# Layer 2 of a two-layer decoder trunk: two heads' projections ahead of the fast-multiplication sets, and head chains begun by a count of steps

## The chip, the cores and the metric

The kernel runs on one core of one Trainium2 chip. The metric is device time in microseconds (us) of one launch. Engines are named as in the profile: PE is TensorE's matmuls, PEld its weight loads, DVE VectorE, ACT ScalarE, POOL GpSimd, SP SyncE. SP and POOL also issue the large transfers, each through a queue of its own.

## The reference, cut to what matters

Two layers run on x of 512 positions by 2048 channels. The first (a convolution branch and an attention branch) isn't touched. The second is a gated linear recurrence with 16 heads:

```python
h = rmsnorm(x, od_norm_g)
p = h @ od_w_in                                # 2048 -> 4 x 2048
q, f_raw, i_val, g = _split(p, ...)            # each 16 heads of 128
o = hgrn2(q, f_raw, i_val, lb, hgrn_norm_g) * jax.nn.silu(g)
x = x + o @ od_w_out
return rmsnorm(x, final_norm_g)

# in hgrn2, of each head, in chunks of 64 positions:
logf = logaddexp(log(lb), log1p(-lb) + log_sigmoid(f_raw))
k = -expm1(logf)
A = einsum('bhtk,bhsk,bhtsk->bhts', q, k, decay)
o = A @ v + (q * exp(b)) @ state               # then rmsnorm per head
```

Everything is float32 and has to be that accurate, so each matrix product is made of three passes on TensorE over operands that are split into a high and a low part: high by high, high by low, low by high.

## The kernel before, in words

**A quarter.** `mm3` (L221 to L223) issues three matmuls of 128 x 128 by 512 columns. Twelve of them are a quarter: one 128 x 512 strip of weights against four row blocks of x. A weight tile (512 KB, two quarters) comes from one of several makers. `Loaded` (L162, L166, L167) fetches the tile with a transfer of POOL's queue as `wh`, has ACT write its negative to `wl`, and fetches the tile again, added to `wl`: what is left is the low part. `Formed` loads raw blocks through SP, forms sums of them on DVE, and splits them with one ACT and one DVE instruction (L248, L249). The tiles stand in one list, `items`. `begin(n)` makes the second step of tile n + 2 and the first of tile n + 3 whenever tile n is begun, so the work on a tile starts three tiles ahead of its use. High and low parts have four and three slots.

**Ticks.** After each quarter (or product, below) `tick()` lets every running chain make one step. A chain is a Python generator; it emits the small operations of a head, of a mean square and so on, between the big matmuls. `finish(...)` steps the named chains to their end at once, without big matmuls between the steps.

**Order.** TensorE's instructions run in the order in which the code is written. The other engines' are ordered by the framework's scheduler.

**Layer 2 before.** Layer 1's last output projection calls `to_h1(c)` for each of 16 column blocks c: it stores x to DRAM (`xd`, L794), splits it into `h1` (L244, L245) and squares it (L256). Then the projections to v and to the gate come first. They are computed in four sets, from weight blocks of 512 KB, by a Strassen-Winograd scheme: seven half-size products (28 weight tiles, each of 12 matmuls) in place of eight. A set has four passes: A11 and A12 (8 tiles), S1 and S2 (8), S4 and S3 (8), A22 (4), where S1 = A21 + A22, S2 = S1 - A11, S3 = A11 - A21, S4 = A12 - S2 are sums of quadrants of x. The sums are made in the first pass of the first set: `x_sums(k)` (L828 to L836) reloads two blocks of x from `xd`, scales them on ACT, makes four sums on DVE, and splits them; S1 goes into the half of `h1[k]` in which A21 would stand. The first set's tiles of pass one are `Loaded`; all other set tiles are `Formed`. Before the third pass of the last set `restore()` (L757) loads A21 back and splits it into `h1`, since the heads need the whole of x.

Then the 16 heads follow: `head(h)` computes the queries ("oq", 4 quarters, L1098) and the decays ("of", 4 quarters, L1102 to L1107), and spawns the chain `hgrn` (L1000 to L1087; 14 steps, the last of them the four transposes of L1087, which wait for `on`, the gated output, L1083). The output projection `w_out` is done by groups of four heads. Group 0 is spread over heads 5 to 7 and group 1 over heads 9 to 11, after a `finish` of the heads that they need; group 2 comes after head 15. The loading of x for the residual (`load_xa`) is spawned at the start of the heads.

Of the kernel before, what the change touches and what calls it, by code (L numbers as in the profile page):

```python
# [49 lines left out]
def trunk(ctx: ExitStack, tc: tile.TileContext, x, w, ws, vec, cst, rope, msk, out, order):  # L50
# [622 lines left out]
    ph = [None]  # L673
# [52 lines left out]

    for s_ in range(len(SETS)):
        for m in range(4):
            if s_ == 0:
                items.append(Loaded(ws[0, 0, 0, m]))  # L730
                items.append(Loaded(ws[0, 1, 0, m]))
            else:
                items.append(Formed(lambda s_=s_, m=m: t1_raw(s_, m), lambda r: r[0], lambda r, s_=s_, m=m: t1_sum(s_, m)))
                items.append(Formed(lambda s_=s_, m=m: block(s_, 1, 0, m), lambda r: r))
# [15 lines left out]
    for i in range(N_EARLY, N_WTILES):  # L750
        items.append(Loaded(w[i]) if 2 * i < LAST else Kept(w[i], 2 * i - LAST))
# [10 lines left out]
    with ectx as cctx:  # L762
# [60 lines left out]
    def x_sums(k):  # L823

        t = ring("xr")
        u = t.rearrange("p (a c) -> p a c", a=2)
        for a in range(2):
            nc.sync.dma_start(u[:, a, :], xd[:, k + 8 * a, :])  # L828
            act.activation(u[:, a, :], u[:, a, :], AF.Copy, scale=vs[:, V_ODG + k + 8 * a:V_ODG + k + 8 * a + 1])
        a11, a21, a12, a22 = u[:, 0, :H], u[:, 0, H:], u[:, 1, :H], u[:, 1, H:]  # L830
        q = ring("xs")
        s1, s2, s3, s4 = [q[:, i * H:(i + 1) * H] for i in range(4)]
        dve.tensor_tensor(out=s1, in0=a21, in1=a22, op=ALU.add)
        dve.tensor_tensor(out=s2, in0=s1, in1=a11, op=ALU.subtract)
        dve.tensor_tensor(out=s3, in0=a11, in1=a21, op=ALU.subtract)
        dve.tensor_tensor(out=s4, in0=a12, in1=s2, op=ALU.subtract)  # L836
        split_plain(s1, h1[k][0][:, H:], h1[k][1][:, H:])
        split_plain(q[:, H:], *sums[k])

    def operand(name, k):  # L840
        if name in ("A11", "S1"):
            return [t[:, (name == "S1") * H:][:, :H] for t in h1[k]]
        if name in ("A12", "A22"):
            return [t[:, (name == "A22") * H:][:, :H] for t in h1[k + 8]]
        i = int(name[1]) - 2
# [21 lines left out]
    rh = fp.tile([P, 4], F32, name="rh")  # L867
# [17 lines left out]
    def keep(tag, b):  # L885
        return fp.tile([P, S], F32, name=tag, tag=f"{tag}{b}")

    for s_ in range(4):
        p1, p2 = banks(), banks()
        for m in range(4):  # L890
            product(p1, "A11", m)
            if s_ == 0:
                x_sums(2 * m)
                t1_raw(0, m)
            product(p2, "A12", m)
            if s_ == 0:
                x_sums(2 * m + 1)
                t1_sum(0, m)
        if s_ == 0:
            finish(c1)  # L900
            dve.tensor_scalar(rh, r1, 0.5, None, op0=ALU.mult)
# [6 lines left out]
        for m in range(4):  # L908
            product(p5, "S1", m)
            product(p6, "S2", m)  # L910
        u = [keep("u", b) for b in range(2)]
# [5 lines left out]
        if s_ == 3:  # L917
            restore()
# [7 lines left out]
        for b in range(2):  # L926
            result(s_, 1, 2 + b, p7[b], u[b])
        p4 = banks()
# [10 lines left out]
    spawn(load_xa(xd))  # L939
# [151 lines left out]
    heads = []  # L1091

    def head(h, fill):
        gate = tp.tile([P, S], F32, name="gate", tag="gate", bufs=2)
        nc.sync.dma_start(gate.rearrange("p (b c) -> p b c", b=4), gd[h // 4][:, :, blocks(h % 4)])
        ps = dense("oq", h, h1)
        q = hgt("q")
# [171 lines left out]
```

## Time and profile before

| | us |
|---|---|
| median of three runs (1833.5 to 1834.43) | 1834.14 |
| the profiled execution | 1832.11 |
| its span, first to last instruction | 1830.2 |
| PE busy, of the span | 1753.9 (96%) |
| DVE busy | 1193.8 (65%) |
| ACT busy | 734.6 (40%) |
| POOL busy | 239.2 (13%) |
| chain of waits: PE's share of the span | 83% |

The mean granted TensorE clock of the run is 0.976 of full speed (2.4 GHz; the lower level, 0.50, is 1.2 GHz). An engine's busy time says nothing on the rate at which TensorE worked: at the lower clock a matmul is busy twice as long. So a stretch of a program in which TensorE is the bound loses two things, the idle time, and half of the time that it was busy at the lower clock. Both are read from one row of a table by stretches: the width less the busy time times the granted clock.

### The profile page before, as it was taken

To read this page: it belongs to the slowest core of one execution; us is meant where nothing else is said; L and a number is where in the kernel's file an instruction comes from. 1 tells how busy PE (TensorE), PEld (TensorE's weight loads), DVE (VectorE), ACT (ScalarE), POOL (GpSimd) and SP (SyncE) were. 2 spreads that over 40 slices of the span, in tenths; PEclk is the share of its full clock that TensorE was granted. 3 is DMA by queue.
4 is the path that set the end of the run, shared out by engine and by line. 5 is a ranking of instruction groups with operands and counts; after the bars stand their busy time and mean duration, and the time that the engine had idled before them with its cause. 6 is when DMAs were issued, how large, how long until landed. Compare 5 with 4: busy or idle time off the path is not lost.

```text
span 1830.2 us, 22277 instructions
## 1 busy us (share of the span) xinstructions
PE 1753.9 (96%) x8227; PEld 1451.7 (79%) x8227; DVE 1193.8 (65%) x2258; ACT 734.6 (40%) x1345; POOL 239.2 (13%) x310
## 2 busy tenths in 40 slices
PE   8999999999999999976999999899899899999997
PEld 6888888888788888854888887788688788878887
DVE  8554867586799765647777786266555555556766
ACT  6334444443433322545454554233233323223344
POOL 5000000000000000340000000222122222222200
PEclk9999999999999999987999999999899999999998
DMA  6222222222552232498676775977577867877752
GB/s 235 83 93 87 89 89 88 92 86 93 182 158 93 94 102 98 155 264 250 205 227 230 203 225 154 296 170 162 133 160 167 181 148 167 168 168 155 155 136 93
DMA packets 96524, 280.68 MB, mean 153 GB/s; under 512 B 9632, under 2 KB 23200, under 8 KB 95520
## 3 DMA queue, kind: packets, MB, share of 16 engines
q0 software_dynamic: 29952, 109.07, 28.1%
q1 hardware_dynamic: 65888, 169.24, 27.3%
q8 instruction: 64, 1.05, 0.2%
q10 hardware_dynamic: 576, 0.97, 0.2%
q14 instruction: 44, 0.36, 0.1%
HBM read 259.31 MB, written 19.92 MB: 153 GB/s over the span
## 4 chain that ended last, share of the span: by engine, by line
PE 83%; DVE 6%; DMA 5%; issue 3%; ACT 2%; POOL 1%; POOLq 0%; DVEq 0%; ACTq 0%; SPq 0%
PE mm L223 23%; PE mm L222 23%; PE mm L221 23%; PE aux L988 2%; PE aux L222 2%; PE aux L221 2%; PE aux L223 2%; DMA rw<-ws 2%; PE aux L454 1%; DVE wl L249 1%; PE aux L1035 1%; DVE hl L245 1%; DMA wh<-w 1%; DMA wl<-w 1%; DVE wq L249 1%
## 5 line engine op out<-in xcount | busy, mean ns | idle before, releaser
L248 ACT ACTIVATE wq<-raw 128x512 fp32r<-128x512 f32 x256 | 161.0, 631 | 351.0 <-PE mm L223 341.5
L221 PE MATMUL mm<-hh,wq 128*128 128x512 f32 x656 | 263.0, 401 | 2.3 <-ACT wq L248 2.3
L249 DVE TENSOR_TENSOR wq<-raw,wq 128x512 fp32r<-128x512 f32 x256 | 183.7, 720 | 120.1 <-ACT wq L248 119.5
L223 PE MATMUL mm<-hh,wq 128*128 128x512 f32 x656 | 257.4, 392 | 2.8 <-DVE wq L249 2.8
L222 PE MATMUL mm<-hl,wq 128*128 128x512 f32 x656 | 256.8, 391 | 0.0
L166 ACT ACTIVATE wl<-wh 128x1024 fp32r<-128x1024 f32 x96 | 101.6, 1058 | 298.8 <-PE mm L223 249.9
L221 PE MATMUL mm<-hh,wh 128*128 128x512 f32 x512 | 210.1, 410 | 0.0
L223 PE MATMUL mm<-hh,wl 128*128 128x512 f32 x512 | 203.3, 397 | 6.4 <-DMA wl<-w 6.4
L222 PE MATMUL mm<-hl,wh 128*128 128x512 f32 x512 | 202.7, 396 | 0.0
L503 DVE SCALAR_TENSOR_TENSOR y<-u,cwh,y 128x512 f32<-128x512 f32 x240 | 178.7, 749 | 2.4
L223 PEld LDWEIGHTS mm<-hh,wq 128*128 128x128 f32 x656 | 123.8, 189 | 30.4 <-DVE wq L249 3.9
L221 PEld LDWEIGHTS mm<-hh,wq 128*128 128x128 f32 x656 | 124.3, 190 | 27.9 <-ACT wq L248 2.8
L222 PEld LDWEIGHTS mm<-hl,wq 128*128 128x128 f32 x656 | 124.2, 189 | 25.9 <-DVE hl L245 0.5
L223 PEld LDWEIGHTS mm<-hh,wl 128*128 128x128 f32 x512 | 98.0, 191 | 29.0 <-DMA wl<-w 7.4
L222 PEld LDWEIGHTS mm<-hl,wh 128*128 128x128 f32 x512 | 98.4, 192 | 18.8
L221 PEld LDWEIGHTS mm<-hh,wh 128*128 128x128 f32 x512 | 98.5, 192 | 18.5
L664 DVE TENSOR_TENSOR xall<-xall,mm 128x512 f32<-128x512 f32 x96 | 65.7, 684 | 67.6 <-PE mm L223 67.5
L221 PE MATMUL mm<-mh,wq 128*128 128x512 f32 x256 | 101.6, 397 | 0.0
L222 PE MATMUL mm<-ml,wq 128*128 128x512 f32 x256 | 101.3, 396 | 0.0
L223 PE MATMUL mm<-mh,wq 128*128 128x512 f32 x256 | 101.2, 395 | 0.0
L162 POOL DMA_DIRECT2D wh<-w x88 | 49.7, 565 | 334.2 <-PE mm L223 288.1
L167 POOL DMA_DIRECT2D wl<-w x88 | 76.8, 873 | 95.1 <-ACT wl L166 88.6
(309 smaller groups left out, 3627.1 us busy)
## 6 DMA issues: line engine op xcount, KB each, us to landing
raw<-w SPq DMA_DIRECT2D x127, 512.0 KB, 3.3
rw<-ws SPq DMA_DIRECT2D x92, 512.0 KB, 4.7
wh<-w POOLq DMA_DIRECT2D x88, 512.0 KB, 3.7
wl<-w POOLq DMA_DIRECT2D x88, 512.0 KB, 6.0
ts<-ws POOLq DMA_DIRECT2D x16, 512.0 KB, 5.6
xall<-xT SPq DMA_DIRECT2D x16, 256.0 KB, 4.7
xd<-xall SPq DMA_DIRECT2D x16, 256.0 KB, 2.5
wh<-ws POOLq DMA_DIRECT2D x8, 512.0 KB, 6.9
```

What stands on the lines that cost most here:

```text
L162: pool.dma_start(self.hi, self.src)
L166: act.activation(self.lo, self.hi.bitcast(F32), AF.Copy, scale=-1.0)
L167: pool.dma_start(self.lo, self.src, accum_op=ALU.add)
L221: pe.matmul(ps, a[0][:, asl], b[0][:, bsl], start=first, stop=False)
L222: pe.matmul(ps, a[0][:, asl], b[1][:, bsl], start=False, stop=False)
L223: pe.matmul(ps, a[1][:, asl], b[0][:, bsl], start=False, stop=last)
L245: dve.scalar_tensor_tensor(out=lo, in0=src, scalar=g, in1=hi.bitcast(F32), op0=ALU.mult, op1=ALU.subtract)
L248: act.activation(hi, src, AF.Copy)
L249: dve.tensor_tensor(out=lo, in0=src, in1=hi.bitcast(F32), op=ALU.subtract)
L503: dve.scalar_tensor_tensor(out=y, in0=u[:, j:j + S], scalar=cwh[:, w0 + j:w0 + j + 1], in1=y, op0=ALU.mult, op1=ALU.add)
L664: dve.tensor_tensor(out=xa[c], in0=xa[c], in1=ps, op=ALU.add)
L988: pe.matmul(ps[:, i * 192:(i + 1) * 192], ks[:, blocks(g)], rhs, start=True, stop=True)
```

## The change

Three things change in layer 2; what is computed stays, up to the order of the same products.

1. *Two heads first.* Queries and decays of heads 0 and 1 (16 quarters) come right after layer 1, before the sets. Their eight tiles are `Loaded`; the first set's pass-one tiles become `Formed` like those of the other sets. `x_sums` runs under head 0's quarters and takes x from where it still stands on the chip, without loads; it makes S1, S2 and S4. The finished queries and key factors go to DRAM (`qd`) and come back when the heads start.
2. *S3 takes S1's place.* S3 is made by `x_diff` in the first and second pass of the first set, from four loads of 512 KB, and is what stands in the half of `h1`. So `restore()` can come after the third pass of the last set, before the fourth. The first two tiles of the heads after the sets are loaded by SP and split on ACT and DVE (`plain`).
3. *Chains by count.* A hook, called at every tick, begins the next head's chain 8 ticks after the last one (10 for the sixth to the twelfth), provided that its q and k are there. The queries and decays of a head therefore run one or two heads ahead of its chain. `w_out` of group 0 is spread over heads 6 to 9 and of group 1 over heads 9 to 12.

```diff
+    hooks = []
     def tick():
+        for f in hooks:
+            f()
         for g in list(chains):
...
+    for i in range(N_EARLY, N_EARLY + 8):
+        items.append(Loaded(w[i]))
     for s_ in range(len(SETS)):
         for m in range(4):
-            if s_ == 0:
-                items.append(Loaded(ws[0, 0, 0, m]))
-                items.append(Loaded(ws[0, 1, 0, m]))
-            else:
...
+    for i in range(N_EARLY + 8, N_WTILES):
+        if i < N_EARLY + 10:
+            items.append(Formed(lambda i=i: plain(i), lambda r: r))
...
     def x_sums(k):
-        t = ring("xr")
-        u = t.rearrange("p (a c) -> p a c", a=2)
+        u = xt.tile([P, 2, S], F32, name="xr", tag="xr", bufs=2)
         for a in range(2):
-            nc.sync.dma_start(u[:, a, :], xd[:, k + 8 * a, :])
-            act.activation(u[:, a, :], u[:, a, :], AF.Copy, scale=...)
+            act.activation(u[:, a, :], xa[k + 8 * a], AF.Copy, scale=...)
...
-        dve.tensor_tensor(out=s3, in0=a11, in1=a21, op=ALU.subtract)
         dve.tensor_tensor(out=s4, in0=a12, in1=s2, op=ALU.subtract)
-        split_plain(s1, h1[k][0][:, H:], h1[k][1][:, H:])
-        split_plain(q[:, H:], *sums[k])
+        split_plain(q, *sums[k])
+    def x_diff(i):
+        t = ring("xr")
+        u = t.rearrange("p (a c) -> p a c", a=2)
+        nc.sync.dma_start(u, xd[:, 2 * i:2 * i + 2, :])
+        for j in range(2):
+            k = 2 * i + j
+            dve.tensor_tensor(out=u[:, j, :H], in0=u[:, j, :H], in1=u[:, j, H:], op=ALU.subtract)
+            split_scaled(u[:, j, :H], vs[...], h1[k][0][:, H:], h1[k][1][:, H:])
+    for h in range(2):
+        ps = dense("oq", h, h1)
+        if h == 0:
+            for k in range(4):
+                x_sums(k)
+            finish(c1)
...
+        nc.sync.dma_start(qd[h][:, 0, :], z)
+        ps = dense("of", h, h1)
...
+        nc.sync.dma_start(qd[h][:, 1, :], decay(h, ps, ...))
...
-        if s_ == 3:
-            restore()
         for m in range(4):
             product(p3, "S4", m)
             product(p7, "S3", m)
...
+        if s_ == 3:
+            restore()
         p4 = banks()
...
-    spawn(load_xa(xd))
...
+    SPREAD = {0: [(6, 1, 3), (7, 0, 3), (7, 1, 3), (8, 0, 3), (8, 1, 2), (9, 0, 2)],
+              1: [(9, 1, 3), (10, 0, 3), (10, 1, 3), (11, 0, 3), (11, 1, 2), (12, 0, 2)]}
+    def begin_chain():
+        since[0] += 1
+        n = len(heads)
+        if n < begun[0] and since[0] >= (8 if n < 5 else 10 if n < 12 else 8):
+            since[0] = 0
+            start(n)
+    hooks.append(begin_chain)
...
+    for h in range(2, 16):
+        if h == 4:
+            spawn(load_xa(xd))
         ps = dense("oq", h, h1)
+        q, kn = qk_tiles(h)
         dve.tensor_tensor(out=q, in0=ps, in1=rb1, op=ALU.mult)
+        out_part(h, 0)
+        decay(h, dense("of", h, h1), kn)
+        begun[0] = h + 1
+        out_part(h, 1)
```

How the change moves instructions is seen at three places. The first is SP's queue where layer 2 begins (`xd` is the stored x, `rw` a raw weight block of a set, `xr` the reloaded x, `qd` the stored queries and key factors). Before:

```order
L794 DMA xd<-xall 128x512 x10
L828 DMA xr<-xd 128x512 x2
L710 DMA rw<-ws 128x1024 x2
L828 DMA xr<-xd 128x512 x2
L710 DMA rw<-ws 128x1024
```

and now:

```order
L813 DMA xd<-xall 128x512 x10
L873 DMA qd_6618<-z 128x512
L881 DMA qd_6618<-gate 128x512
L714 DMA rw<-ws 128x1024 x4
L873 DMA qd_6619<-z 128x512
L714 DMA rw<-ws 128x1024 x7
L881 DMA qd_6619<-gate 128x512
L714 DMA rw<-ws 128x1024
L857 DMA xr<-xd 128x1024
```

The sixteen reloads of 256 KB that stood between the weight blocks are gone; two stores of 256 KB for each of two heads stand there, twelve weight blocks among and behind them, and the first of four reloads of 512 KB.

The second place is ACT where a head's chain ends and `w_out` of its group is near: head 3 (`kst`, `st`, `on` and `mh` are the chain's last steps, `wl` the second step of a `Loaded` tile, `pi` and `xe` the start of the next chain). Before:

```order
L1054 ACTIVATE kst<-aux 128x384
L1008 ACTIVATE xe<-f 128x128
L1060 ACTIVATE st<-aux 128x128
L1073 ACTIVATE on,ss<-aux 128x128 x4
L1082 ACTIVATE on<-aux,rs_10280 128x128 x4
L976 ACTIVATE ab<-pi 128x16
L977 ACTIVATE ab<-pi 128x16
L976 ACTIVATE ab_10471<-ab 128x4
L977 ACTIVATE ab_10471<-ab 128x4
L244 ACTIVATE mh<-aux,hgn 128x512
L166 ACTIVATE wl<-wh 128x1024 x5
```

and now:

```order
L170 ACTIVATE wl<-wh 128x1024
L1092 ACTIVATE kst<-aux 128x384
L1098 ACTIVATE st<-aux 128x128
L1014 ACTIVATE ab_10600<-ab 128x4
L1015 ACTIVATE ab_10600<-ab 128x4
L170 ACTIVATE wl<-wh 128x1024
L1111 ACTIVATE on,ss<-aux 128x128 x4
L1120 ACTIVATE on<-aux,rs_10486 128x128 x4
L1045 ACTIVATE pi<-f 128x128
L1046 ACTIVATE xe<-f 128x128
L170 ACTIVATE wl<-wh 128x1024
L248 ACTIVATE mh<-aux,hgn 128x512
```

The last steps of the chain stood one behind the other, without a tile's `wl` between them; now a `wl`, thus two quarters of big matmuls, stands between the steps.

The third place is DVE at the end of the last set (`z`, `gate` and `v` are results of the set, `wl` of `ts` the low parts of the fourth pass's tiles, `hl` the low parts of the restored half of x). Before:

```order
L882 SCALAR_TENSOR_TENSOR gate<-th,gate 128x512
L875 TENSOR_TENSOR z<-mm,u 128x512
L875 TENSOR_TENSOR gate<-aux,u 128x512
L249 TENSOR_TENSOR wl<-ts,wh 128x1024
L882 SCALAR_TENSOR_TENSOR z<-th,z 128x512
L249 TENSOR_TENSOR wl<-ts,wh 128x1024
L882 SCALAR_TENSOR_TENSOR gate<-th,gate 128x512
L875 TENSOR_TENSOR z<-aux,v 128x512
L875 TENSOR_TENSOR gate<-aux,v 128x512
```

and now:

```order
L926 SCALAR_TENSOR_TENSOR gate<-th,gate 128x512
L919 TENSOR_TENSOR z<-mm,u 128x512
L919 TENSOR_TENSOR gate<-aux,u 128x512
L249 SCALAR_TENSOR_TENSOR hl_6343<-xr,vs,hh_6342 128x256
L926 SCALAR_TENSOR_TENSOR z<-th,z 128x512
L249 SCALAR_TENSOR_TENSOR hl_6368<-xr,vs,hh_6367 128x256
L253 TENSOR_TENSOR wl<-ts,wh 128x1024
L926 SCALAR_TENSOR_TENSOR gate<-th,gate 128x512
L253 TENSOR_TENSOR wl<-ts,wh 128x1024
L253 TENSOR_TENSOR wl<-rw,wh 128x1024 x2
```

Two of the restored low parts and a gating step now stand ahead of the third `wl` of the fourth pass.

## Rows read from the trace of the kernel before

**Rows 1.** The page, part 2: granted clock in tenths, 40 slices of 45.8 us
```profile
PEclk9999999999999999987999999999899999999998
```

**Rows 2.** Stretches: width, busy us of PE PEld DVE ACT POOL, clock, DMA share, GB/s
```profile
790.00:880.00 90.00, 59.65 (x223) 46.30 (x222) 51.88 (x82) 46.00 (x61) 12.98 (x16) 0.79 0.88 258
1112.00:1122.00 10.00, 7.80 (x27) 5.80 (x26) 7.08 (x6) 4.50 (x5) 0.00 (x0) 0.83 0.16 54
1142.00:1166.00 24.00, 17.62 (x65) 13.69 (x64) 3.07 (x5) 5.46 (x6) 5.03 (x8) 0.86 1.08 318
1284.00:1302.00 18.00, 9.36 (x40) 7.77 (x39) 14.29 (x41) 6.47 (x24) 2.54 (x4) 0.72 0.50 132
1456.00:1472.00 16.00, 10.35 (x49) 8.65 (x48) 12.97 (x34) 6.82 (x23) 3.07 (x5) 0.79 0.60 160
1632.00:1644.00 12.00, 8.85 (x29) 6.91 (x28) 6.15 (x22) 3.55 (x10) 3.04 (x5) 0.72 0.52 113
```

**Rows 3.** TensorE's first product of layer 2: start us, us
```profile
788.88 0.39 PE L221 MATMUL mm<-wh,hh 128*128 128x512 f32 x1
```

**Rows 4.** ScalarE reads a set's seventh product, set 1 and set 2
```profile
927.47 0.60 ACT L904 ACTIVATE v<-aux 128x512 f32<-128x512 f32 x1 [3.70 <-PE aux L223]
...
1003.63 0.60 ACT L904 ACTIVATE v<-mm 128x512 f32<-128x512 f32 x1 [3.03 <-PE mm L223]
```

**Rows 5.** VectorE reads the decays of heads 2 and 3
```profile
1226.36 0.69 DVE L1102 TENSOR_TENSOR z<-mm,rb 128x512 f32<-128x512 f32 x1 [2.46 <-PE mm L223]
...
1254.80 0.69 DVE L1102 TENSOR_TENSOR z<-mm,rb 128x512 f32<-128x512 f32 x1 [2.46 <-PE mm L223]
```

**Rows 6.** Waits, 780 to 880 us: engine, line, waited for; us, times, longest
```profile
ACT wl L166 <- DMA wh<-ws: 15.4, 5, 7.6
...
PE aux L221 <- ACT wh L248: 13.6, 2, 11.6
PE mm L222 <- DMA wl<-ws: 12.9, 4, 7.0
```

**Rows 7.** DMA issues, 770 to 880 us: KB each, median us to landing
```profile
wl<-ws POOLq DMA_DIRECT2D x8, 512.0 KB, 8.5
...
wh<-ws POOLq DMA_DIRECT2D x7, 512.0 KB, 8.1
```

**Rows 8.** DMA issues, 1300 to 1500 us
```profile
wh<-w POOLq DMA_DIRECT2D x29, 512.0 KB, 3.6
wl<-w POOLq DMA_DIRECT2D x29, 512.0 KB, 6.0
```

**Rows 9.** Costs by line and form, 780 to 880 us: busy, mean ns
```profile
L829 ACT ACTIVATE xr<-xr,vs 128x512 f32<-128x512 f32 x16 | 11.0, 712 | 5.1 <-DMA xr<-xd 4.9
...
L249 DVE TENSOR_TENSOR fl<-xs,fh 128x768 fp32r<-128x768 f32 x8 | 7.6, 954 | 1.2 <-ACT fh L248 1.2
...
L248 ACT ACTIVATE fh<-xs 128x768 fp32r<-128x768 f32 x8 | 6.7, 835 | 2.5 <-DVE xs L836 2.5
...
L833 DVE TENSOR_TENSOR xs<-xr 128x256 f32<-128x256 f32 x8 | 3.4, 423 | 2.1 <-ACT xr L829 1.9
```

**Rows 10.** TensorE's waits, 780 to 1770 us
```profile
PE aux L1087 <- DVE on L1083: 10.9, 4, 5.5
...
PE aux L1087 <- DVE ab L979: 3.2, 1, 3.2
```

**Rows 11.** Stretches of 2 us after a longer and about a short wait
```profile
1118.00:1120.00 2.00, 2.00 (x6) 1.52 (x6) 1.23 (x1) 0.26 (x1) 0.00 (x0) 0.50 0.00 0
1162.00:1164.00 2.00, 1.30 (x6) 0.82 (x5) 0.62 (x1) 0.00 (x0) 0.51 (x1) 1.00 1.10 339
1164.00:1166.00 2.00, 2.00 (x11) 1.63 (x10) 0.00 (x0) 1.06 (x1) 0.00 (x0) 1.00 1.08 247
```

**Rows 12.** VectorE at head 12: second reciprocal of its chain, gating of head 11
```profile
1629.64 1.69 DVE L1018 RECIPROCAL rc<-pi 128x256 f32<-128x256 f32 x1
...
1635.62 0.69 DVE L1083 TENSOR_TENSOR on<-on,gate 128x512 f32<-128x512 f32 x1
```

More of the change, by code (lines that the diff above doesn't have):

```diff
@@ L823, in x_sums @@
     def x_sums(k):
+        u = xt.tile([P, 2, S], F32, name="xr", tag="xr", bufs=2)
+        for a in range(2):
+            act.activation(u[:, a, :], xa[k + 8 * a], AF.Copy, scale=vs[:, V_ODG + k + 8 * a:V_ODG + k + 8 * a + 1])
+        a11, a21, a12, a22 = u[:, 0, :H], u[:, 0, H:], u[:, 1, :H], u[:, 1, H:]
+        q = xt.tile([P, 3 * H], F32, name="xs", tag="xs")
+        s1, s2, s4 = [q[:, i * H:(i + 1) * H] for i in range(3)]
+        dve.tensor_tensor(out=s1, in0=a21, in1=a22, op=ALU.add)
@@ L891, in trunk @@
             product(p1, "A11", m)
-            if s_ == 0:
-                x_sums(2 * m)
-                t1_raw(0, m)
             product(p2, "A12", m)
[L896 to L901, printed above, removed]
+            if s_ == 0 and m % 2:
+                x_diff(m // 2)
         v = [keep("v", b) for b in range(2)]
@@ L910, in trunk @@
             product(p6, "S2", m)
+            if s_ == 0 and m % 2:
+                x_diff(2 + m // 2)
         u = [keep("u", b) for b in range(2)]
@@ L1091, in trunk, with qk_tiles, start @@
     heads = []
-    def head(h, fill):
+    qk = {}
+    def qk_tiles(h):
+        qk[h] = (hg.tile([P, S], F32, name="q", tag="q", bufs=2), tmp("m", bufs=1) if h % 2 else hgt("kn"))
+        return qk[h]
+    def start(h):
         gate = tp.tile([P, S], F32, name="gate", tag="gate", bufs=2)
         nc.sync.dma_start(gate.rearrange("p (b c) -> p b c", b=4), gd[h // 4][:, :, blocks(h % 4)])
+        q, kn = qk[h]
+        heads.append(spawn(hgrn(h, kn, q, gate)))
+    for h in range(2):
+        for i, t in enumerate(qk_tiles(h)):
+            nc.sync.dma_start(t, qd[h][:, i, :])
@@ new lines, in trunk, with out_part @@
+    SPREAD = {0: [(6, 1, 3), (7, 0, 3), (7, 1, 3), (8, 0, 3), (8, 1, 2), (9, 0, 2)],
+              1: [(9, 1, 3), (10, 0, 3), (10, 1, 3), (11, 0, 3), (11, 1, 2), (12, 0, 2)]}
+    begun = [2]
+    since = [99]
+    def begin_chain():
[5 more added lines that the diff above has]
+    hooks.append(begin_chain)
+    def out_part(h, i):
+        for g, parts in SPREAD.items():
+            c = 0
+            for part in parts:
+                if part[:2] == (h, i):
+                    if c == 0:
+                        finish(*heads[:4 * g + 4])
+                    w_out("ow", list(range(4 * g, 4 * g + 4)), range(c, c + part[2]))
+                c += part[2]
@@ L1108, in head @@
-        heads.append(spawn(hgrn(h, kn, q, gate)))
-        w_out("ow", *fill[1])
-    for h in range(16):
-        g, j = divmod(h, 4)
-        rows = list(range(4 * g - 4, 4 * g))
-        fill = [(rows, range(0))] * 2
-        if g in (1, 2) and j:
-            finish(*heads[:4 * g])
-            c = [0, 3, 5, 8, 10, 13, 16]
-            fill = [(rows, range(c[2 * j - 2 + i], c[2 * j - 1 + i])) for i in range(2)]
-        head(h, fill)
+        out_part(h, 0)
+        decay(h, dense("of", h, h1), kn)
@@ L1120, in trunk @@
+        begun[0] = h + 1
+        out_part(h, 1)
     w_out("ow", [8, 9, 10, 11], range(NK))
+    assert len(heads) == 16
     finish(*heads)
```

71 lines of the change are left out of this document (39 added, 32 removed).

## The prediction

> **What bounds the kernel now.** I read the page's clock row first. It should stand at 9 all along in a kernel that TensorE bounds, and it dips in slices 18, 19, 29 and the last [rows 1]: at 778 to 869 us, where layer 2 begins, at 1281 to 1327, and at the end, which the change leaves alone. In a dip TensorE has just waited, and works at half speed afterwards. So I went on to the table by stretches, once coarsely over layer 2, then closely around each hole; six remain [rows 2]. What a stretch lost is its width less busy time times granted clock:
>
> - seam to layer 2: 90 - 59.65 x 0.79 = 42.9 us
> - restore in the fourth set: 10 - 7.80 x 0.83 = 3.5
> - first head: 24 - 17.62 x 0.86 = 8.8
> - ahead of head 5: 18 - 9.36 x 0.72 = 11.3
> - ahead of head 9: 16 - 10.35 x 0.79 = 7.8
> - head 12: 12 - 8.85 x 0.72 = 5.6
>
> Together 79.9 us. The largest can be counted in another way. Two sets in sequence read their seventh product 1003.63 - 927.47 = 76.16 us apart [rows 4]; that is 2.72 us for each of 28 products, and this is the pace without waits. Layer 2 began at 788.88 [rows 3], so the seventh product of the first set was due at 788.88 + 7 x 2.72 = 807.9. One set before 927.47 is 851.3. That gives 43.4 lost, as the stretches say.
>
> Then I read who ended the waits. At the seam TensorE waited 12.9 us for the added transfer of `Loaded` low parts, and 13.6 for ScalarE's `wh`; ScalarE itself stood 15.4 us waiting for `wh` transfers [rows 6]. So it is the transfers: they took 8.1 and 8.5 us to land there [rows 7], against 3.6 and 6.0 where only the heads' tiles are fetched [rows 8]. At heads 5 and 9 TensorE's transposes waited 10.9 us for `on`, at head 12 3.2 us for other VectorE work [rows 10]: a chain stepped to its end with nothing between, and a chain caught behind the next one's reciprocals.
>
> The matmuls stay the same in number and shape, and all engines but TensorE have slack. So the change is worth what it takes of these 79.9 us, less what it leaves or adds.
>
> **The seam (42.9 us).** Sixteen quarters of 2.72 us, 43.5 us, now stand where the four passes began. Under them x_sums needs of ScalarE 8 x (2 x 0.712 + 0.835) = 18.1 us and of VectorE 8 x (3 x 0.423 + 0.954) = 17.8 us [rows 9]: the subtraction and the split that went are small, and both engines have less than half of the stretch to do. The sixteen reloads of 256 KB are gone from it, and the first set's tiles are no longer fetched twice.
>
> What can be late is a `Loaded` tile. It is begun three tiles, 3 x 5.44 = 16.3 us, ahead. With 3.6 + 6.0 to land and an estimated 2 us for ScalarE and the issue it takes 11.6 and is in time. With 8.1 + 8.5 it takes 18.6, so a tile could come only every 6.2 us instead of 5.44: 0.8 x 8 = 6 us lost. The two ends are 0 and 6; the weight blocks of the first set are still prefetched in this stretch, but the reloads are gone, so I stand nearer to the quiet row. With a short wait for the mean square, whose chain is finished after four quarters, I take 3 us.
>
> **x_diff and the stores.** Eight subtractions and eight splits of 256 columns, at 0.42 us each by the nearest row [rows 9], are 6.8 us of VectorE in 16 products, 43.5 us. If all of it stood ahead of a low part that TensorE needs, 6.8 would be lost; if the work lies in VectorE's idle time, nothing. Its tiles are begun two or three products ahead, so I take 0.5. The stores and reloads of `qd` (four times 256 KB each way) wait on nothing that TensorE needs: 0. They make SP wait in its queue ahead of weight blocks; those have five buffers to run ahead in.
>
> **Restore (3.5 us).** The two loads go out in the same way, but nothing in the third pass reads them now, and they are wanted only when the heads begin. What is left: two restored low parts and a gating step stand ahead of the third `wl` of the fourth pass, about 2 x 0.42 + 0.7 = 1.5 us of VectorE, half of it covered. I take 0.7, between 0 and the whole 3.5.
>
> **First head (8.8 us).** The first two tiles come by SP and are split, so no double transfer through POOL is waited for. The first `Loaded` one is needed 2 x 5.44 = 10.9 us after the heads begin. The loads of the residual still lie there. Ends are 0 and 8.8; I take 1.5.
>
> **Heads 5 and 9 (19.1 us).** A chain has 14 steps. Begun at ticks 1, 9, 17 and 25, head 3 ends at tick 38; the first `w_out` quarter of group 0 is at tick 41 (five heads of eight quarters before it). Head 7, begun at tick 63, ends at 76; group 1 starts at 81. So both `finish` calls find nothing to step, and each step is followed by a quarter of 2.72 us, in place of the 18 and 16 us stretches without cover. I take 0 for what remains, bounds 0 and 19.1 (the latter only if the counts are wrong).
>
> **Head 12 (5.6 us) and other chains.** The stall came from a reciprocal of 1.69 us and what follows it, ahead of the gating step, which started only at 1635.62 [rows 12]. Where the chains are 8 ticks apart nothing like it happened: heads 2 and 3 finished 28.44 us apart, which is 8 x 2.72 + 6.7 for the chain's own matmuls [rows 5]. With heads 8 and 10 ticks apart most chains now keep clear of each other, but at head 11 a reciprocal still stands ahead of the gating step. I leave 3 us there and 1 for the others together; bounds 0 and, if every chain of sixteen met its successor so, 16 x 5.6 = 90.
>
> The sum: 3 + 0.5 + 0.7 + 1.5 + 0 + 4 = 9.7 stay. 1832.1 of the profiled execution less 79.9 and plus 9.7 is 1761.9; the median of the runs shown stands 2.0 above that execution, so 1764.
>
> **What short waits do to the clock.** After the restore's wait TensorE worked at 0.50 (1.2 GHz); but a wait of 0.70 us left it at 1.00 (2.4 GHz) in that stretch and the next [rows 11]. The Trainium skill (TensorE: Matmul & The Clock Gate, section "HAM oscillation — how this bites in real kernels") says that matmul bursts with transfer waits between them are throttled again at each wait, and so run the start of each burst slowly; the longer waits of this trace agree, the 0.70 us one doesn't. As a mechanism of this kernel: if each of five remaining waits also brings the lower clock, it costs what it cost at head 12, 5.6 less 3.2 idle = 2.4 us, so 12 us in all and 1776.
>
> **The rivals.**
> 1. Transfers stay slow. For it: rows 7, and that the sets' raw blocks, `Loaded` tiles and stores still share the stretch; at the first head the residual's loads too. Against: the sixteen reloads are gone. The seam's other end (6 in place of 2 of the 3 counted) and the first head unchanged (+7.3): 1764 + 11.3 = 1775.
> 2. Chains collide at three or four heads besides 12, as VectorE's order for the early q and k puts tanh, split and reciprocal work ahead of the gating. For it: rows 12. Against: rows 5. 3.5 x 5.6 = 19.6: 1784.
> 3. The seam's loss is half moved rather than removed, the change not doing what it says: weight blocks of the first set, now all raw, come late because SP waits with a `qd` store at the head of its queue. Half of 42.9: 1785.
> 4. The clock as above: 1776.
> 5. Slower. The gating of a head and the reciprocals of the next always meet, since each chain now begins by a fixed count, 8 or 10 ticks after the last, and steps 9 to 13 of one fall on steps 1 to 4 of the next. From 70.2 / 5.6 = 12.5 heads on the gain is gone; at 14 heads 1764 + 78 = 1842. Against it: chains 8 ticks apart did not stall in the heads before 5 [rows 5].
>
> **How the numbers follow.** Forecast 0.55; rivals 1 to 5 in order 0.16, 0.11, 0.07, 0.05, 0.04; 0.02 for a mixture that ends within 0.2%, 3.7 us, which is about what a measurement of this kernel can tell from no change. So faster 0.94, same 0.02, slower 0.04. The forecast's own range is 1754 (nothing stays) to 1774. The whole range goes up to 1788, to take in rivals 1 to 4, and down to 1752, for small waits that I haven't counted.
>
> **What would show it.** Right: the stretch from 789 us on stays at a clock of 1.00 for 43 us with TensorE busy throughout; the first set takes 76 us; `on` is no longer among TensorE's waits; the fourth set's third pass shows no hole; heads 1 to 12 follow each other at 2.72 us a tick plus 6.7 a chain. Wrong: waits for `wl<-w` at the seam (rival 1), for `wl<-rw` or `wh` in the first set (rival 3), transposes waiting for `on` behind reciprocals in many heads (rivals 2 and 5), clock 0.50 after waits under a microsecond (rival 4). A total above 1790 would mean that a term of this sum is missing.

## The result and the profile after

The changed kernel takes 1765.6 us (median of four runs, 1763.4 to 1771.3) where the kernel before takes 1833.9 beside it (1833.5 to 1834.4): a ratio of 0.9632, 95% interval 0.9609 to 0.9655. The forecast was 1764 us. The profiled execution took 1763.39 us, 68.7 less than that of before; the sum in the prediction had 70.2.

The page's clock row, which dipped in slices 18, 19 and 29 [rows 1], now stands at 9 but for the last slice, the end of the program:

```profile
PEclk9999999999999999999999999999999999999998
```

The table by stretches has the columns of [rows 2]. Its first two rows are the seam, now sixteen quarters and the first set's first pass (788 to 868) and the beginning of the second pass (868 to 882). Rows three and four are the places of the restore and of the first head, at the same times as before, since the 43 us that the seam lost are now 43 us of work. The last two are the only kinds of hole among the heads:

```profile
788.00:868.00 80.00, 77.22 (x346) 63.17 (x344) 50.92 (x77) 44.95 (x61) 12.29 (x15) 1.00 0.85 240
868.00:882.00 14.00, 11.48 (x41) 8.78 (x42) 10.36 (x13) 8.27 (x10) 1.71 (x2) 0.88 0.80 210
1112.00:1122.00 10.00, 10.00 (x44) 7.95 (x43) 9.91 (x11) 5.42 (x6) 1.39 (x2) 1.00 0.74 209
1142.00:1166.00 24.00, 24.00 (x112) 20.05 (x111) 20.53 (x46) 7.74 (x14) 5.50 (x9) 1.00 0.86 243
1200.00:1210.00 10.00, 8.88 (x44) 7.24 (x43) 7.87 (x23) 3.94 (x7) 1.95 (x3) 1.00 0.51 109
1560.00:1570.00 10.00, 9.26 (x50) 7.67 (x49) 6.79 (x12) 6.95 (x19) 4.26 (x6) 1.00 0.83 209
```

The losses, as width less busy time times clock: 2.8 us in the first 80, 3.9 at 868 to 882, nothing at the restore and at the first head (10.00 and 24.00 busy at clock 1.00), 1.1 at 1200, which comes four times, and 0.7 at 1565. The first 2.8 are two waits and little else: 1.4 us for the mean square (L283) and 1.2 for a `Loaded` low part (`wl<-w`). TensorE's waits from 770 to 1700 us (engine, line, waited for: us in all, times, longest) are few:

```profile
PE aux L1026 <- DVE X L1012: 4.5, 4, 1.1
PE aux L225 <- ACT wh L252: 1.5, 1, 1.5
PE aux L286 <- DVE c L283: 1.4, 1, 1.4
PE aux L226 <- DVE wl L253: 1.2, 2, 0.8
PE mm L227 <- DMA wl<-w: 1.2, 1, 1.2
PE aux L1125 <- DVE on L1121: 0.7, 1, 0.7
```

The transposes waited 14.1 us for VectorE, 10.9 of them for the gating [rows 10]; 0.7 are left. The `Loaded` tiles under the quarters land in 4.4 and 5.8 us (medians, 780 to 900 us), against 8.1 and 8.5 [rows 7] and near the quiet 3.6 and 6.0 [rows 8]:

```profile
wl<-w POOLq DMA_DIRECT2D x8, 512.0 KB, 5.8
wh<-w POOLq DMA_DIRECT2D x6, 512.0 KB, 4.4
```

The seventh product of the first set and of the second are read 937.41 - 856.84 = 80.6 us apart, 4.4 more than the 76.16 of [rows 4]; most of that is the hole at 868 once more:

```profile
856.84 0.58 ACT L941 ACTIVATE v<-mm 128x512 f32<-128x512 f32 x1
937.41 0.60 ACT L941 ACTIVATE v<-aux 128x512 f32<-128x512 f32 x1 [3.70 <-PE aux L227]
```

### The profile page after: what moved, and what is told of

Same layout as the page of the kernel before. It is cut to its first block, busy times and chain, and to the rows that moved or that the text cites. A ratio compares the mean times of both kernels' runs of the same rounds, so it can differ in the third digit from the quotient of the medians.

```text
span 1761.6 us, 22265 instructions
## 1 busy us (share of the span) xinstructions
PE 1731.8 (98%) x8227; PEld 1436.4 (82%) x8227; DVE 1208.7 (69%) x2268; ACT 735.5 (42%) x1345; POOL 224.2 (13%) x290
## 3 DMA queue, kind: packets, MB, share of 16 engines
q0 software_dynamic: 27072, 98.58, 26.4%
## 4 chain that ended last, share of the span: by engine, by line
PE 86%; DVE 7%; DMA 3%; issue 2%; ACT 2%; POOL 1%; POOLq 0%; DVEq 0%; ACTq 0%
PE mm L225 24%; PE mm L227 24%; PE mm L226 24%; PE aux L226 2%; PE aux L225 2%; PE aux L227 2%; PE aux L1026 2%; DMA rw<-ws 1%; PE aux L458 1%; PE aux L1106 1%; DVE hl L249 1%; DVE wl L253 1%; PE aux L1096 1%; PE aux L1073 1%; DVE wq L253 1%
## 5 line engine op out<-in xcount | busy, mean ns | idle before, releaser
L170 ACT ACTIVATE wl<-wh 128x1024 fp32r<-128x1024 f32 x86 | 90.9, 1057 | 225.3 <-PE mm L227 214.6
L252 ACT ACTIVATE wh<-rw 128x1024 fp32r<-128x1024 f32 x66 | 69.7, 1058 | 79.7 <-DMA rw<-ws 30.1
L253 DVE TENSOR_TENSOR wl<-rw,wh 128x1024 fp32r<-128x1024 f32 x66 | 79.8, 1222 | 18.0 <-ACT wh L252 5.3
```

What stands on the lines that cost most here:

```text
L170: act.activation(self.lo, self.hi.bitcast(F32), AF.Copy, scale=-1.0)
L252: act.activation(hi, src, AF.Copy)
L253: dve.tensor_tensor(out=lo, in0=src, in1=hi.bitcast(F32), op=ALU.subtract)
```

## The experiments

The profile says which holes closed, not which part of the change closed them. The theory at the start was the prediction's: the seam is closed as transfers no longer come late, the restore and the first head by their two edits, the holes at heads 5 and 9 as `finish` finds nothing to step. The main rivals were that one part alone (the reloads, or the early queries) did most of it. Medians are of four runs unless said otherwise, and each ratio is to the kernel before on the same chip.

**Which transfers?** First (e1), x_sums reloads x again, under the quarters:

```diff
-            act.activation(u[:, a, :], xa[k + 8 * a], AF.Copy, scale=...)
+            nc.sync.dma_start(u[:, a, :], xd[:, k + 8 * a, :])
+            act.activation(u[:, a, :], u[:, a, :], AF.Copy, scale=...)
```

> The changed kernel, but x_sums loads its sixteen blocks of 256 KB from DRAM again, as before, under head 0's quarters. Theory: at the seam the transfers were only late because no other work stood over them; under 43.5 us of quarters they cost nothing or little, so 0 to +4 us against the changed kernel (1765.6), clock 1.00 throughout 789 to 830. Rival: the reloads themselves were the cause, as they delay the weight transfers: then wl and wh land in 8 us again, TensorE waits for wl, and +10 us or more.

1768.75 us (1765.3 to 1770.6), ratio 0.9642 (0.9628 to 0.9656): 3 us above the changed kernel, within the spread of both and within the 0 to 4 of my theory. So the reloads don't undo the change. But the theory had the clock at 1.00 throughout, and that failed. The profiled execution, at 1770.57 us the longest of the four, loses 80 - 70.33 x 0.94 = 13.9 us in the stretch in which the changed kernel loses 2.8 (at 868 to 882 it loses nothing, where the changed kernel loses 3.9). Two waits make this hole (the stretch; TensorE's waits, 780 to 900 us):

```profile
788.00:868.00 80.00, 70.33 (x297) 57.28 (x296) 40.64 (x64) 36.70 (x49) 11.46 (x14) 0.94 0.88 257
```

```profile
PE aux L286 <- DVE c L283: 6.5, 1, 6.5
PE mm L227 <- DMA wl<-w: 3.2, 2, 2.8
```

The `Loaded` tiles now land in 6.6 and 6.9 us instead of 4.4 and 5.8, and one of them is waited for. The longer wait is of a kind that neither side expected. The mean square's last matmuls wait 6.5 us for the end of a chain of small instructions (L283). The first of these on VectorE, L275, has its input at 797.9, when the matmuls of L273 end; it starts only at 805.45 (in the changed kernel at 800.43). VectorE took its instructions in order here, and ahead of it stood sums of x, the first of which waited for a reload:

```profile
802.25 0.43 DVE L849 TENSOR_TENSOR xs<-xr 128x256 f32<-128x256 f32 x1 [11.01 <-ACT xr L845]
...
805.45 0.15 DVE L275 TENSOR_SCALAR rm<-aux 128x4 f32<-128x4 f32 x1
```

Taking x from the chip saves this as well.

Second (e4), the first set's first-pass tiles are fetched twice again, with x still taken from the chip:

```diff
+            if s_ == 0:
+                items.append(Loaded(ws[0, 0, 0, m]))
+                items.append(Loaded(ws[0, 1, 0, m]))
+            else:
...
             product(p1, "A11", m)
+            if s_ == 0:
+                t1_raw(0, m)
             product(p2, "A12", m)
+            if s_ == 0:
+                t1_sum(0, m)
```

> The changed kernel, but the eight tiles of the first set's first pass are Loaded (fetched twice through POOL) again, with the raw blocks fetched for the sums besides. Theory: away from the reloads of x these transfers land in some 4 and 6 us, in time: 0 to +4 us against the changed kernel. Rival: fetching twice what is fetched raw as well fills the transfers' capacity, landing times of 8 us and TensorE waits for wl as at the seam before: +8 to +15.

1785.9 us (1780.9 to 1786.2), ratio 0.9738 (0.9722 to 0.9754): +20, more than the rival's 8 to 15. My theory falls here. TensorE waits for `wl` of these tiles, and at 820 to 880 us the DMA engines are busy 1.04 of the time (the column ahead of the last):

```profile
PE mm L226 <- DMA wl<-ws: 14.8, 6, 3.5
```

```profile
820.00:880.00 60.00, 43.92 (x152) 32.77 (x151) 15.95 (x25) 16.35 (x23) 11.63 (x16) 0.83 1.04 314
```

60 - 43.92 x 0.83 = 23.5 us are lost there. VectorE is busy 16 of these 60 us, so it isn't vector work. Fetching twice what is fetched raw as well is six blocks for two products of TensorE; forming the tiles is three. Whether the tiles came late because of these bytes alone, or also because a tile in a set is begun only three products ahead (see e12 below), e4 doesn't separate.

**The restore and the first head alone** (e3), in the kernel before:

```diff
-    for i in range(N_EARLY, N_WTILES):
-        items.append(Loaded(w[i]) if 2 * i < LAST else ...)
+    for i in range(N_EARLY, N_WTILES):
+        if i < N_EARLY + 2:
+            items.append(Formed(lambda i=i: plain(i), lambda r: r))
+        else:
+            items.append(Loaded(w[i]) if 2 * i < LAST else ...)
...
-        if s_ == 3:
-            restore()
         for m in range(4):
             product(p3, "S4", m)
             product(p7, "S3", m)
...
+        if s_ == 3:
+            restore()
         p4 = banks()
```

> The kernel before with two edits alone: restore after the third pass of the last set, and the first two head tiles loaded by SP and split. Theory: the two stretches lose 0.7 and 1.5 instead of 3.5 and 8.8, so -10 us: 1824, no hole at 1114 us, and TensorE does not wait for wl at the first head. Rival: the first head's wait is due to the loads of the residual, which stay there, so only the restore's 3 us go: 1831.

1822.8 us (1821.3 to 1824.2), ratio 0.9939 (0.9924 to 0.9954): -10.3, the sum that the theory had. The two stretches:

```profile
1112.00:1122.00 10.00, 10.00 (x46) 8.29 (x45) 7.62 (x12) 6.76 (x12) 0.00 (x0) 1.00 0.60 195
1142.00:1166.00 24.00, 20.66 (x85) 16.29 (x84) 1.38 (x2) 4.07 (x4) 5.05 (x9) 0.94 1.07 315
```

The restore's hole is gone. At the first head 24 - 20.66 x 0.94 = 4.6 us are still lost, with the DMA share at 1.07: the first two tiles are in time, the third, `Loaded`, isn't, against the theory. So the two stretches give 3.5 + 4.2 = 7.7 us. The profiled execution is 9.8 below that of before; 3.0 of these lie in the first 50 us, which the edits don't touch (9.3 lost before, 6.3 here). In the changed kernel the first head loses nothing, and the DMA share over the same 24 us is 0.86: there the residual's loads go out from 1151.6 us on, in e3 from 1135.6. That the remainder is due to these loads alone was not tried.

**Steps left for `finish`** (e2). Both spread projections are placed one head earlier, so that the chains aren't done:

```diff
-    SPREAD = {0: [(6, 1, 3), (7, 0, 3), (7, 1, 3), (8, 0, 3), (8, 1, 2), (9, 0, 2)],
-              1: [(9, 1, 3), (10, 0, 3), (10, 1, 3), (11, 0, 3), (11, 1, 2), (12, 0, 2)]}
+    SPREAD = {0: [(5, 1, 3), (6, 0, 3), (6, 1, 3), (7, 0, 3), (7, 1, 2), (8, 0, 2)],
+              1: [(8, 1, 3), (9, 0, 3), (9, 1, 3), (10, 0, 3), (10, 1, 2), (11, 0, 2)]}
```

> The changed kernel with both spread output projections placed one head (8 ticks) earlier, so that finish has steps left: head 3 ends at tick 38 and the first quarter of group 0 is at tick 33, head 7 ends at 76 and group 1 starts at 73. Theory: the steps that are left run without big matmuls between them, and the losses ahead of heads 5 and 9 of the kernel before come back: +15 to +20 us (11.3 + 7.8 if in full), TensorE waiting for the gating of L1121 and for VectorE's steps. Rival: the early queries and keys, not the finish, took these losses away: less than +4.

1785.2 us (1784.4 to 1786.4), ratio 0.9734 (0.9720 to 0.9749): +19.6. The wait for the gating is back, and the stretches about the two `finish` calls lose 20 - 15.11 x 0.74 = 8.8 and 16 - 8.69 x 0.94 = 7.8 us:

```profile
PE aux L1125 <- DVE on L1121: 11.4, 3, 5.8
```

```profile
1268.00:1288.00 20.00, 15.11 (x60) 12.61 (x59) 6.06 (x21) 4.62 (x17) 3.04 (x5) 0.74 0.28 91
1408.00:1424.00 16.00, 8.69 (x47) 7.00 (x46) 8.96 (x20) 6.00 (x19) 2.89 (x5) 0.94 0.71 187
```

The queries and keys were as early as in the changed kernel, so it is the ticks between the last chain and `w_out` that pay.

**What the seam was made of.** After the miss on the tiles I took the seam of the kernel before apart. First without reloads of x (e8):

```diff
-            nc.sync.dma_start(u[:, a, :], xd[:, k + 8 * a, :])
-            act.activation(u[:, a, :], u[:, a, :], AF.Copy, scale=...)
+            act.activation(u[:, a, :], h1[k + 8][0].bitcast(F32), AF.Copy, scale=...)
```

> The kernel before without the sixteen reloads of x at the seam: x_sums copies from the split blocks that are on the chip instead (the sums are then of other blocks). Theory now: the first pass was bound by the bytes that it fetches. At the seam 8 tiles were fetched twice (8.4 MB), 8 raw blocks besides (4.2 MB) and x (4.2 MB); the profiled stretch 790 to 870 moved 269 GB/s in the mean, some 21.5 MB. Without 4.2 MB the loss falls by 4.2 / 0.27 = 15 us, to 28: about 1818. Rival: the reloads sit between the weight blocks in SP's queue and hold the sums up, and are the main cause: the loss falls under 10 us, 1798. Second rival: they are hidden, no change.

1818.5 us (1815.0 to 1822.3), ratio 0.9921 (0.9890 to 0.9952): -14.5, the size that the bytes gave. But the edit also takes away what the sums waited for these reloads [rows 9], so this run alone can't tell one from the other. Then also four of the eight tiles formed (e10):

```diff
-            if s_ == 0:
+            if s_ == 0 and m < 2:
                 items.append(Loaded(ws[0, 0, 0, m]))
                 items.append(Loaded(ws[0, 1, 0, m]))
...
-                t1_raw(0, m)
+                if m < 2:
+                    t1_raw(0, m)
...
-                t1_sum(0, m)
+                if m < 2:
+                    t1_sum(0, m)
```

> As the last, and of the first set's eight first-pass tiles the last four are formed from raw blocks that serve the sums as well, so fetched once instead of twice and once more. That saves 6 blocks of 512 KB, 3.1 MB. By bytes: another 3.1 / 0.27 = 12 us off, 16 us of loss left, about 1806. Rival (only the order in the queues counts): as e8 within 3 us.

1825.4 us (seven runs, 1824.3 to 1828.5), ratio 0.9959 (0.9946 to 0.9972): not 12 us less but 7 more, though the bytes went. So bytes are not the whole of it. In stretches of 20 us from 790 on, e8 first (VectorE is the third busy number, DMA share the one ahead of the last), then e10:

```profile
790.00:810.00 20.00, 12.96 (x53) 9.90 (x52) 10.44 (x25) 11.10 (x17) 7.16 (x10) 0.83 1.03 301
810.00:830.00 20.00, 12.15 (x48) 9.19 (x47) 17.94 (x33) 15.23 (x24) 1.28 (x2) 0.86 0.85 243
830.00:850.00 20.00, 16.67 (x63) 12.70 (x63) 12.72 (x16) 9.45 (x11) 2.59 (x3) 0.89 0.81 237
```

```profile
790.00:810.00 20.00, 10.95 (x47) 8.28 (x46) 10.38 (x19) 8.57 (x13) 4.26 (x5) 0.84 0.92 276
810.00:830.00 20.00, 16.59 (x66) 12.60 (x64) 14.94 (x30) 14.05 (x23) 0.00 (x0) 0.90 0.37 126
830.00:850.00 20.00, 11.04 (x36) 7.58 (x36) 16.90 (x26) 13.38 (x18) 0.93 (x1) 0.87 0.66 214
```

In e8 the first stretch has a DMA share of 1.03 and the second a VectorE busy 17.9 of 20 us. In e10 at 810 to 850 the DMA engines are half idle (0.37 and 0.66) while VectorE is busy 14.9 and 16.9 of 20: forming tiles needs VectorE, and the sums need it too. The kernel before has such a stretch already, and in it TensorE's longest wait, of 11.6 us for ScalarE's `wh` [rows 6], ended at 846.32:

```profile
830.00:850.00 20.00, 7.97 (x28) 5.80 (x28) 17.16 (x29) 14.74 (x22) 0.86 (x1) 0.67 0.68 229
```

To tell, the sums were made once instead of eight times, first with all tiles fetched twice (e11), then with half of them (e12):

```diff
-                x_sums(2 * m)
+                if m == 0:
+                    x_sums(0)
...
-        return [t[:, i * H:(i + 1) * H] for t in sums[k]]
+        return [t[:, i * H:(i + 1) * H] for t in sums[0]]
```

> e8 (the kernel before, no reloads of x), and the sums of x are made for one pair of blocks alone and used for all, so that seven eighths of the sums' ScalarE and VectorE work are gone; the tiles are still fetched twice. In e8 VectorE was busy 9.7 of 10 us at 820 to 830, in e10 10 of 10 at 830 to 840, where transfers were few. Theory: the seam had two limits one behind the other, the bytes in its first half, the vector work in its second. Then the loss falls by another 8 to 12 us against e8's 1818, to 1806 to 1810, and what remains are waits for wl from DRAM. Rival: only bytes count, and the tiles fetched twice set the end: no change against e8, 1818.

> e11 with the last four of the eight first-pass tiles formed from the raw blocks (3.1 MB fewer, as in e10). Theory of two limits: with neither the work of the sums nor these bytes, the seam loses 8 to 14 us of its 43: 1798 to 1804, and against e11 the saving of bytes now gains 4 to 10 us, where in e10 it gained none. Rival: changing over from the one kind of tile to the other costs a wait of its own, which made e10 slower: as e10, 1820 or more, with its wait of 8 us for wl at 800.

e11 takes 1812.8 us (1811.0 to 1814.3), ratio 0.9883 (0.9869 to 0.9897); e12 takes 1807.0 (1806.0 to 1809.9), ratio 0.9854 (0.9841 to 0.9868). Both went the way of the two limits. From e8 to e11 it is 5.7 us, less than the 8 to 12 that I had expected, and the intervals of the two overlap. From e11 to e12 it is 5.7 again, within the 4 to 10 expected, though e12 stands 3 us above its 1798 to 1804. The seam's own rows separate more than the totals; e8, e10, e11 and e12:

```profile
790.00:880.00 90.00, 69.89 (x284) 54.71 (x283) 61.70 (x92) 48.65 (x64) 11.89 (x15) 0.91 0.84 241
790.00:880.00 90.00, 66.90 (x264) 51.54 (x263) 62.76 (x93) 48.52 (x64) 7.77 (x9) 0.89 0.65 197
790.00:880.00 90.00, 72.43 (x304) 58.60 (x303) 47.59 (x54) 36.40 (x41) 13.42 (x17) 0.89 0.85 253
790.00:880.00 90.00, 78.00 (x333) 63.28 (x332) 57.61 (x64) 39.99 (x45) 6.69 (x7) 0.92 0.77 233
```

They lose 26.4, 30.5, 25.5 and 18.2 us, against 42.9 before (summed over rows of 10 us from 780 to 900: 25.2, 29.0, 22.7 and 15.3, against 40.9). With the sums in, fetching less costs some 4 us; with the sums left out, it gains 7. With all tiles fetched twice, leaving out the sums gains 1 to 3; with half of them formed, it gains 12 to 14 (of 18 in the totals). So each of the two limits hides the other. The rest of the differences lies outside the seam, where the restore and the first head are above all, and was not explained (1080 to 1180 us: e8 loses 100 - 89.04 x 0.93 = 17.2, e11 100 - 91.28 x 0.97 = 11.5). What e11 waits for is `wl` alone:

```profile
PE mm L222 <- DMA wl<-ws: 17.6, 4, 8.4
```

And e12 still has one wait of 8.4 us. It is the fourth tile's. POOL issues its first transfer at 789.07, the second at 798.41, and TensorE goes on at 808.12 (POOL, then PE: start, us):

```profile
789.07 0.61 POOL L162 DMA_DIRECT2D wh<-ws  x1
...
798.41 0.87 POOL L167 DMA_DIRECT2D wl<-ws  x1 [6.72 <-ACT hh L248]
```

```profile
808.12 0.79 PE L222 MATMUL mm<-wl,hh 128*128 128x512 f32 x1 [8.44 <-DMA wl<-ws]
```

POOL's second transfer waits for ScalarE, which makes `wl` only at 797.06, as the first transfer has landed. The tile took 19 us from its first step. In a set a tile lasts one product, 2.72 us, so three tiles ahead are 8.2 us; under quarters they are 16.3. The fourth tile is the first whose lead is made of set products alone, and it is late in all five of these kernels: TensorE waits 7.0 us for it before, 5.4 in e8, 7.9 in e10, 8.4 in e11 and e12. That would be a third limit of the old seam, its start. It is argued and not shown: no run began these tiles earlier with all else the same, and in e12 each transfer still took about 8 us.

**The two holes that the change left.** x_diff with a buffer of its own instead of places in the ring (e5):

```diff
-        t = ring("xr")
-        u = t.rearrange("p (a c) -> p a c", a=2)
-        nc.sync.dma_start(u, xd[:, 2 * i:2 * i + 2, :])
         for j in range(2):
             k = 2 * i + j
+            t = ph[0].tile([P, S], F32, name="xr", tag="xr")
+            nc.sync.dma_start(t, xd[:, k, :])
```

> The changed kernel, whose first set loses some 4 us at 868 to 882 us, where a raw block that SP issued at 865.5 comes late. x_diff gets a buffer of its own (one block of 256 KB at a time, eight loads instead of four), so that it takes no place in the ring of five that prefetches the raw blocks. Theory: the ring's places taken by x_diff cost the prefetch; the hole goes, -4 us against the changed kernel (1765.6), to about 1762. Rival: x_diff's work on VectorE and ScalarE, or SP's wait for the store of z ahead of the block, makes the hole; it stays.

1762.9 us (1758.7 to 1764.6), ratio 0.9614 (0.9590 to 0.9637): inside the changed kernel's interval. The hole is still there, 14 - 12.45 x 0.88 = 3.0 us at 866 to 880 (changed kernel: 14 - 11.24 x 0.92 = 3.7):

```profile
866.00:880.00 14.00, 12.45 (x47) 9.57 (x46) 11.38 (x13) 8.24 (x10) 1.72 (x2) 0.88 0.98 213
```

So not the ring. The second reciprocal in two halves (e6):

```diff
-        dve.reciprocal(blk(rc, 1), blk(pi, 1))
+        for i in range(2):
+            n = slice(32 * i, 32 * i + 32)
+            dve.reciprocal(blk(rc, 1)[:, n], blk(pi, 1)[:, n])
```

> The changed kernel with the second reciprocal of a head's chain (1.75 us on VectorE) in two halves. At 8 ticks from chain to chain it stands ahead of the last X product (0.23 us) of the head before, for which TensorE waits 1.1 us in four heads. With the halves in VectorE's order one stands ahead and one behind. Theory: these four waits fall to about 0.3 us each, -3 us against the changed kernel, about 1762.5; no other wait changes. Rival: the wait only moves to a later step of the chain (qb, the next products): no change within 1 us in the profile.

1761.3 us (1759.3 to 1762.5), ratio 0.9607 (0.9587 to 0.9627). This interval overlaps the changed kernel's, so the gain is read from the profile. The four waits fall from 4.5 to 1.2 us, from 1.1 to 0.3 each, and none longer than 0.3 us has come in their place:

```profile
PE aux L1026 <- DVE X L1012: 1.2, 4, 0.3
```

And last, with this, x_diff away from the end of the first pass (e13):

```diff
             product(p2, "A12", m)
-            if s_ == 0 and m % 2:
-                x_diff(m // 2)
+            if s_ == 0 and m < 2:
+                x_diff(m)
...
-            if s_ == 0 and m % 2:
-                x_diff(2 + m // 2)
+            if s_ == 0 and m == 3:
+                x_diff(2)
...
             product(p7, "S3", m)
+            if s_ == 0 and m == 0:
+                x_diff(3)
```

> The changed kernel with the split reciprocal of e6, and x_diff moved away from the end of the first pass: its four calls stand after the first and second pair of products of pass one, at the end of pass two and after the first pair of pass three. e5 showed that the hole at 868 to 882 us is not made by the ring; the rival left is that x_diff's vector work there (ScalarE 8.7, VectorE 8.4 of 10 us at 860 to 870 in the changed kernel) comes on top of the results of the pass. Theory: the hole closes by half or more: 2 to 3 us below e6's 1761.3, so 1758 to 1760. Rival: the hole is SP's, whose store of z stands ahead of the raw block: no change, 1761.

1759.0 us (five runs, 1754.8 to 1759.9), ratio 0.9585 (0.9570 to 0.9599), clear of the changed kernel's interval, but not of e6's. The hole at 866 to 880, which costs 2.0 us in e6, is closed (e6, then e13):

```profile
866.00:880.00 14.00, 11.99 (x52) 9.39 (x51) 10.48 (x14) 8.39 (x12) 1.26 (x3) 1.00 0.88 236
866.00:880.00 14.00, 14.00 (x63) 11.60 (x62) 9.63 (x11) 7.86 (x10) 1.72 (x2) 1.00 0.88 207
```

But its waits show what it got for that: one of 1.3 us for a low part at 890 to 900, where e6 loses nothing, and the mean square's matmuls wait 1.7 us instead of 1.3. (The 3.5 us of L286 include the final mean square.)

```profile
890.00:900.00 10.00, 8.73 (x39) 6.88 (x38) 7.50 (x10) 4.19 (x6) 0.00 (x0) 1.00 0.71 253
```

```profile
PE aux L286 <- DVE c L283: 3.5, 3, 1.7
PE mm L226 <- DVE wl L253: 1.5, 2, 1.3
```

So most of the 2.0 us is lost again elsewhere, and that e13 is faster than e6 is not shown. What is shown is that x_diff's place made the hole at 866 to 880, and not the store of z alone, which stands ahead of the raw block as before. Whether x_diff did it by its vector work or by its loads in SP's queue was not separated.

## Why the prediction was right, point by point

**The holes and their sum.** Six stretches were to give back 79.9 us and 9.7 were to stay. By the profile of after 2.8 + 3.9 + 0 + 0 + 4 x 1.1 + 0.7 = 11.8 stay, and 1832.1 - 79.9 + 11.8 = 1764.0 against a measured 1763.4. The way of counting, width less busy time times clock, holds to a microsecond in the profiled execution. That the forecast came so close owes something to luck: x_diff left 3.4 us more than I had put and the chains 1.1 more, the restore and the first head 2.2 less and the seam 0.2 less. One of my signs failed: the first set took 80.6 us and not 76.

**The seam: right in size, wrong in its cause.** I left 3 us, and 2.8 are left. But "so it is the transfers" was too simple. I put both of TensorE's waits down to transfers that land in 8 us instead of 4 and 6. The longer one, for ScalarE's `wh`, lies where VectorE is busy 17.2 of 20 us and the DMA share is 0.68. The old seam had two limits that hide each other: transfers (without the reloads 16.5 us less are lost at the seam, e8) and the work of the sums on ScalarE and VectorE (12 to 14 us there, from e10 to e12). There was probably a third, the start of the tiles: 16.3 us is a `Loaded` tile's lookahead under quarters, as I used it, but in a set it is 8.2, less than the 11.6 that I had myself reckoned for quiet transfers. Taking away the reloads gave 14.5 us; fetching 3.1 MB less on top of it left 7.6 (e10), since forming the tiles added work to the other limit.

What closes the seam now is three things together: 43 us of work whose tiles last twice as long, x taken from the chip, and tiles fetched once. Under the same quarters, the reloads put back cost 3 us in the median and 11 at the seam of the profiled execution (e1), the double fetch 20 (e4). No run had the quarters alone, or all tiles fetched once without them.

**x_diff: mis-sized.** I took 0.5 of an interval from 0 to 6.8; 3.9 came. The step that failed is "its tiles are begun two or three products ahead", from which I took it that the work would lie in VectorE's idle time. At the end of a pass the results come on top; e13 shows that x_diff moved away from there costs nothing at this place, but 1.3 us at 890 to 900. Of the 3.9 us, 11.48 x 0.12 = 1.4 are the clock, which stood at 0.50 at 878 to 880 (below).

**Restore and first head: right for the restore, in part for the head.** 0.7 and 1.5 were left, 0 and 0 came. In the kernel before, the two edits alone close the restore's hole and half of the first head's (e3). I wrote that the residual's loads still lie at the first head; in the changed kernel `load_xa` is spawned two heads later, and its loads begin 16 us later than in e3, which may be what closes the other half.

**Heads 5 and 9: right.** The count of ticks held, and e2 shows the price of taking it away: 19.6 us, against 19.1 in the sum.

**Other chains: the place was wrong.** I left 3 us at head 12 and 1 for all others; 0.7 and 4.5 came. The step that failed: chains 8 ticks apart did not stall before [rows 5], so I let them keep clear. But a chain now begins by the count and not behind its own decays, so it meets its predecessor elsewhere; that is read from the order, not tried. In four heads a reciprocal of 1.75 us stands ahead of a product of 0.23 for which TensorE waits (VectorE, then PE):

```profile
1199.83 1.75 DVE L1056 RECIPROCAL rc<-pi 128x256 f32<-128x256 f32 x1
1201.49 0.23 DVE L1012 TENSOR_TENSOR X<-X,ab 128x128 f32<-128x128 f32 x1
```

```profile
1201.86 1.38 PE L1026 MATMUL aux<-X,ks 128*128 128x192 f32 x7 [1.12 <-DVE X L1012]
```

That is rival 2 in kind, with another instruction and a fifth of the price: 1.1 us for 5.6, because the wait is short and the clock stays. Dividing the reciprocal took these waits away (e6).

**The rivals.** Rival 1: the transfers did not stay slow (4.4 and 5.8 us); one wait of 1.2 us for `wl<-w` is left. Rival 3: half of the seam's loss did not come back elsewhere. Rival 4, the clock: four single waits of 1.1 us each left it at 1.00 in their stretch. But after two waits of 1.5 and 0.8 us close behind each other it stood at 0.50, at 878 to 880 (the number ahead of the DMA share):

```profile
874.00:876.00 2.00, 0.50 (x1) 0.19 (x1) 1.55 (x4) 1.84 (x3) 0.00 (x0) 1.00 0.71 166
876.00:878.00 2.00, 1.47 (x6) 1.20 (x7) 2.00 (x4) 1.51 (x3) 0.14 (x1) 0.92 0.38 152
878.00:880.00 2.00, 2.00 (x7) 1.52 (x5) 1.53 (x3) 1.34 (x2) 0.72 (x1) 0.50 0.43 45
```

The Trainium skill (TensorE: Matmul & The Clock Gate, section "HAM oscillation — how this bites in real kernels") has matmul bursts throttled again at each transfer wait between them; the waits in its example are of 3 to 5 us. None of the changed kernel's waits here was that long, so the single ones don't speak against it. After the pair the clock did fall, though both waits were shorter; but in e6 waits of 1.3 and 0.8 us at the same place left it at 1.00 (e6's row at 866 to 880 above). Rival 5: no head's gating meets the next head's reciprocals, but for 0.7 us at 1565.

## What to carry to other kernels

A stretch where the bound engine starves may have several limits in series, so removing one shows only the difference to the next, or a loss. A block of work put over them can take most of the stretch, if it doesn't itself need what is short there (e4). Count lookahead in time and not in tiles: three tiles were 16 us in one loop and 8 in the next. And give a chain of small steps as many ticks as it has steps before something asks for its end: a forced finish cost 8 to 11 us each.

## What the runs showed that I had not expected

Fewer bytes made the kernel slower: e10 moves 3.1 MB fewer than e8 and takes 7 us longer, 4 of them at the seam, as its tiles need VectorE (busy 16.9 of 20 us) at the time when the sums do. And a small instruction of 0.15 us started 7.5 us after its input was there, behind one that waited for a transfer (e1).
